# Weights-stationary products of a hybrid decoder trunk: two matmuls of 512 and 256 columns, or three of 256

## The chip, the core and the metric

One core of a Trainium2 chip runs the whole kernel. The metric is the device time of one execution in microseconds; the median of three runs is given. All inputs are in HBM at the start, and the output is in HBM at the end. The engines are TensorE (PE, whose weight loads the profile lists apart as PEld), VectorE (DVE), ScalarE (ACT), GpSimd (POOL) and SyncE (SP), which here issues the loads.

## The reference

256 tokens of width 2048 go through two layers, all in float32:

```python
for i in range(DEPTH):                       # DEPTH = 2
    hn = rms_norm(h, norm_mix[i])
    y = dsa_attention(hn, ...) if i % 2 == 0 else mlstm_mixer(hn, ...)
    h = h + y
    hn = rms_norm(h, norm_ffn[i])
    h = h + jnp.square(jax.nn.relu(hn @ ffn_w_up[i])) @ ffn_w_down[i]   # 2048 -> 8192 -> 2048
```

The attention has 16 heads of 128 with four key heads and an indexer that keeps 64 keys a token; the mLSTM has eight heads with keys and queries of 128 and values of 256. Most of the arithmetic is in the products with weights: 391 MB of them are loaded in a run.

## The kernel before

A product in float32 is made of three products of a faster type (`float32r`). Each operand is split into a high part, which that type holds exactly, and a low part, the rest. Of the four partial products high x high, high x low and low x high are kept. `weights` (L138) loads 512 rows and up to 512 columns of a weight by SyncE, in two tiles of 256 rows, and `split` (L134) makes the high part `wh` on ACT (L135) and the low part `wl` on DVE (L136). The tiles rotate: five for the loads, four each for the parts. `pair` tiles hold both parts of two blocks of 128 rows of the activations against all 256 tokens: `[P, 2 parts, 2 blocks, T]`.

There are two forms of product. `project` (L151) keeps the activations on the array and streams up to 512 columns of a weight (L166 to L168); it yields tokens on the partitions. `project_t` (L174) keeps a block of 128 x 128 of the weight on the array and streams the tokens; it yields the weight's columns on the partitions, 512 of them a call, as four blocks of 128. It is used for FFN up (two layers x four quarters x four calls) and for the mLSTM's keys and queries (four calls).

In `project_t` one call has four accumulators of a whole PSUM bank each, `[P, 2, T]`. For each of 16 blocks of rows and each of four blocks of columns, L191 streams the high and the low part of the activations side by side (512 columns) against the high part of the weight, into both halves of the bank. L193 then streams the high part of the activations (256 columns) against the low part of the weight, into the second half alone. The result is the sum of the two halves. The calls take their banks in turn from the pool `pa` (four banks, which `project` uses too) and from `px` (four banks, the helpers' pool `aux`, for transposes and small products); in the profile these accumulators are `acc` and `acx`.

The eviction adds the halves. In the FFN, `evac_up` (L457) runs for each block of 128 columns: ACT copies the second half out (L462), DVE adds the first (L463), DVE makes the squared relu (L464), and `split` makes the two parts of `hT`, ACT the high and DVE the low. In the mLSTM, `keep` (L580) does the copy and the addition (L582, L583) for `kT` and `qT`.

An FFN layer has four quarters of 2048 hidden columns: four calls of `project_t`, then four calls of `project` with 512 output columns each over the eight `hT` pairs. Each call of the latter has 16 blocks x 2 token tiles x 3 = 96 matmuls. The order of work on each engine is made by a scheduler from the program and a model of times; TensorE executes its matmuls in that order. The squares' scale (the token's factor of the norm) is put on at the very end, so that the products need not wait for the norm.

Of the kernel before, what the change touches and what calls it, by code (L numbers as in the profile page):

```python
# [9 lines left out]
F32 = mybir.dt.float32  # L10
# [27 lines left out]
def trunk_kernel(ctx: ExitStack, tc, x, norm_mix, norm_ffn, att_w_in, att_q_gain, att_k_gain,  # L38
# [16 lines left out]
    def uid(s):  # L55
        n[0] += 1
        return f"{s}_{n[0]}"

    def pair(name):
        """The exact high and low parts of two blocks of 128 rows against all tokens."""  # L60
        return lp.tile([P, 2, 2, T], F32R, tag="pair", name=uid(name))

    def t2k(shape, dt=F32, name="t2k"):
# [23 lines left out]
        nc.tensor.transpose(pg[:, :32], g, ident[:32, :32])  # L87
        nc.vector.tensor_copy(gains[:, col:col + 32], pg[:, :32])

    # TensorE's clock comes up while the first loads run.  # L90
    warm = aux()
    for _ in range(8):
        nc.tensor.matmul(warm[:, :P], zero, zero, start=True, stop=True)
# [25 lines left out]
    nc.gpsimd.memset(one0[:, 1:2], 0.0)  # L119

    def rsqrt(a, cols):
        """1/sqrt of [P, cols] (in place of a tile's values), by Newton's method from a bit-level seed."""
        seed = small([P, cols], I32, "seed")
        y = small([P, cols], F32, "y")
        u = small([P, cols], F32, "u")
        nc.vector.tensor_scalar(seed, a.bitcast(I32), 1, None, op0=ALU.logical_shift_right)
        nc.vector.tensor_scalar(y.bitcast(I32), seed, -1.0, float(0x5F3759DF), op0=ALU.mult, op1=ALU.add)
        for _ in range(3):
            nc.vector.tensor_tensor(u, a, y, op=ALU.mult)
            nc.vector.scalar_tensor_tensor(u, u, -0.5, y, op0=ALU.mult, op1=ALU.mult)  # L130
            nc.vector.scalar_tensor_tensor(y, u, 1.5, y, op0=ALU.add, op1=ALU.mult)
        return y

    def split(hi, lo, src):  # L134
        nc.scalar.copy(hi, src)  # L135
        nc.vector.tensor_tensor(lo, src, hi.bitcast(F32), op=ALU.subtract)  # L136

    def weights(src, k0, n0, width):  # L138
        """Rows k0.. (four blocks of 128) and columns n0..n0+width of a weight, as exact high and low parts."""
        parts = []  # L140
        for i in range(2):
            w = wp.tile([P, 2, 512], F32, tag="w", name=uid("w"), bufs=5)
            r0 = k0 + 256 * i
            nc.sync.dma_start(w[:, :, :width], src[r0:r0 + 256, n0:n0 + width].rearrange("(k p) f -> p k f", p=P))
            wh = wp.tile([P, 2, 512], F32R, tag="wh", name=uid("wh"), bufs=4)
            wl = wp.tile([P, 2, 512], F32R, tag="wl", name=uid("wl"), bufs=4)
            split(wh[:, :, :width], wl[:, :, :width], w[:, :, :width])
            parts.append((wh, wl))
        return parts

    def project(lhs, src, k0, n0, width, evac, before=None):  # L151
        """evac(m, psum): tokens of tile m against columns n0..n0+width. before(g) makes tiles 2g and 2g+1 of lhs."""
        acc = [pa.tile([P, 512], F32, tag="acc", name=uid("acc")) for _ in range(2)]
        nk = 2 * len(lhs)
        for g in range(nk // 4):
            if before is not None:
                before(g)
            for i, (wh, wl) in enumerate(weights(src, k0 + 512 * g, n0, width)):
                a = lhs[2 * g + i]
                for m in range(2):  # L160
                    ms = slice(m * P, (m + 1) * P)
                    o = acc[m][:, :width]
                    for j in range(2):
                        k = 4 * g + 2 * i + j
                        ah, al = a[:, 0, j, ms], a[:, 1, j, ms]
                        nc.tensor.matmul(o, ah, wh[:, j, :width], start=(k == 0), stop=False)  # L166
                        nc.tensor.matmul(o, ah, wl[:, j, :width], start=False, stop=False)  # L167
                        nc.tensor.matmul(o, al, wh[:, j, :width], start=False, stop=(k == nk - 1))  # L168
        for m in range(2):
            evac(m, acc[m][:, :width])  # L170

    turn = [0]

    def project_t(lhs, src, n0, evac):  # L174
        """evac(b, psum): block b of 128 columns from n0 on, on the partitions, against all tokens; the product
        is the sum of the two halves of psum [128, 2, T]."""
        turn[0] ^= 1
        if turn[0]:
            acc = [pa.tile([P, 2, T], F32, tag="acc", name=uid("acc")) for _ in range(4)]
        else:  # L180
            acc = [px.tile([P, 2, T], F32, tag="aux", name=uid("acx")) for _ in range(4)]
        nk = 2 * len(lhs)
        for g in range(nk // 4):
            parts = weights(src, 512 * g, n0, 512)
            for kk in range(4):
                k = 4 * g + kk
                wh, wl = parts[kk // 2]
                a = lhs[k // 2]
                for j in range(4):
                    js = slice(j * P, (j + 1) * P)  # L190
                    nc.tensor.matmul(acc[j], wh[:, kk % 2, js], a[:, :, k % 2], start=(k == 0), stop=False,  # L191
                                     skip_group_check=True)
                    nc.tensor.matmul(acc[j][:, 1], wl[:, kk % 2, js], a[:, 0, k % 2], start=False,  # L193
                                     stop=(k == nk - 1), skip_group_check=True)
        for b in range(4):
            evac(b, acc[b])

    class Norm:
        """The stationary operand of a normed stream, without its tokens' factors; those come out of finish()."""

        def __init__(self, col):
            self.col = col
# [7 lines left out]
                                     accum_out=self.ss[:, m, c:c + 1])  # L210

        def chunk(self, c, squares=None):
            """squares: None for this chunk's own, True for those of all chunks, False for none."""
            for i in (2 * c, 2 * c + 1):
                p = aux()
                for j in range(2):
# [27 lines left out]
            return self  # L244

    def rope_cols(slab, v, heads, half, c0):
        """Turn the first 2*half columns of each head of v [P, 2, heads, d]."""
        rot = 2 * half
        shape = [P, 2, heads, rot]
        a = slab(shape, "ropa")  # L250
# [8 lines left out]
        nc.vector.tensor_tensor(v[:, :, :, :rot], a, b, op=ALU.add)  # L259

    def add_to_h(norm, r2=None):
        """Adds a product's columns to the stream, and hands them to the next norm."""

        def at(c):
            def evac(m, p):
# [8 lines left out]
        return at  # L274

    def slabs(pool, bufs):
        """Tiles of one phase: bufs by tag."""
        return lambda shape, name, tag=None: pool.tile(shape, F32, tag=tag or name, bufs=bufs[tag or name],
                                                       name=uid(name))

    # ---------------------------------------------------------------- attention
    def attention(nm, nxt, pool):
        slab = slabs(pool, {"v": 1, "kT": 1, "qT": 3, "hn": 3, "sq": 2, "ropa": 1, "ropb": 1, "lg": 5, "pT": 3, "sc": 4})
        lhs = nm.lhs
# [86 lines left out]
            bias.append(b)  # L371

        def heads_t(dst, gain):
            """evac of four heads of 128 columns: normed, turned and transposed into dst [P, 4, T]."""
            o = slab([P, 2, 4, DH], "hn")

            def evac(m, p):
# [71 lines left out]
            project(oT, w_ao, 0, 512 * c, 512, at(c))  # L449
        nxt.finish()  # L450

    # ---------------------------------------------------------------- feed-forward
    def ffn(nm, up, down, nxt, last=False):
        for q in range(4):
            hT = []

            def evac_up(b, p):  # L457
                if b % 2 == 0:
                    hT.append(pair("hT"))
                a = hT[-1]  # L460
                u = t2k([P, 2, T], F32, "u")
                nc.scalar.copy(u[:, 0], p[:, 1])  # L462
                nc.vector.tensor_tensor(u[:, 0], p[:, 0], u[:, 0], op=ALU.add)  # L463
                nc.vector.scalar_tensor_tensor(u[:, 1], u[:, 0], 0.0, u[:, 0], op0=ALU.max, op1=ALU.mult)  # L464
                split(a[:, 0, b % 2], a[:, 1, b % 2], u[:, 1])

            for c in range(4):
                project_t(nm.lhs, up, q * 2048 + 512 * c, evac_up)
# [13 lines left out]
        if nxt is not None:  # L482
            nxt.finish()

    # ---------------------------------------------------------------- mLSTM
    def mlstm(nm, nxt, pool):
        slab = slabs(pool, {"go": 4, "mkT": 1, "mqT": 1, "mv": 2, "num": 2, "gT": 1, "row": 1, "et": 2, "pt": 2,
                            "mjunk": 2, "hs": 3})
# [4 lines left out]
        HD = MH * MV  # L493

        def put_o(m, c0, p, width):
            """sigmoid(o) times the heads' gain, for columns c0.. of o."""
            done = 0
            while done < width:
                c = c0 + done
# [17 lines left out]
        e = small([P, 2, MH], F32, "e")  # L517
        nc.vector.scalar_tensor_tensor(e, fg, -1.0, fg, op0=ALU.mult, op1=ALU.min)
        nc.scalar.activation(e, e, AF.Exp)
        # log(1 + e) as log(u) + (e - (u - 1)) / u, with u the rounded 1 + e.  # L520
        u = small([P, 2, MH], F32, "u1")
        ru = small([P, 2, MH], F32, "ru")
        nc.vector.tensor_scalar(u, e, 1.0, None, op0=ALU.add)
# [18 lines left out]
        nc.vector.tensor_tensor_scan(mm, cs, one0[:, 1:2].to_broadcast([MH, T]), 0.0, op0=ALU.max, op1=ALU.max)  # L542
        negm = slab([MH, T], "negm", "hs")
        nc.vector.scalar_tensor_tensor(negm, cum, -1.0, mm, op0=ALU.mult, op1=ALU.subtract)
        # Rows 0.. and 32.. of parts are the exact high and low parts of -mm; pick adds the two of one head.
        parts = pool.tile([40, T], F32R, tag="parts", bufs=1, name="parts")
        pick = cp.tile([40, MH], F32R, name="pick")
        nc.vector.tensor_tensor(pick, ident[:40, :MH], ident[:40, 32:32 + MH], op=ALU.add)
# [27 lines left out]
        for half in range(2):  # L576
# [2 lines left out]

            def keep(dst):  # L580
                def evac(b, p):
                    nc.scalar.copy(dst[:, b], p[:, 1])  # L582
                    nc.vector.tensor_tensor(dst[:, b], p[:, 0], dst[:, b], op=ALU.add)  # L583
                return evac

            project_t(lhs, w_ml, MK0 + 512 * half, keep(kT))
# [84 lines left out]


def _rope_table():
    """By position: [cos cos | -sin sin] of the attention's rotation, then the indexer's."""
    import numpy as np
    cols = []
    for rot in (RC, IC):
# [29 lines left out]
```

## Time and profile before

| | |
|---|---|
| Median of 3 runs | 2126.35 us (2126.17 to 2127.8) |
| Profiled execution, first to last instruction (span) | 2124.9 us |
| PE busy | 2115.0 us, 100%, 10748 records |
| PEld busy | 1810.0 us, 85%, 10748 records |
| DVE, ACT busy | 1242.6 us (58%), 1010.1 us (48%) |
| DMA | 393.09 MB, mean 185 GB/s |

The profile is of one execution, whose own time is known as its span; the runs' times include what lies around that. Times in the rows are microseconds from the span's start, and the means of one instruction are in ns. Matmuls are pipelined: the record of one is longer than the step from its start to the next one's, and its end is modelled. Steps between starts, and counts, are therefore what a rate is read from. A float32 matmul that is not of the split type shows as two records.

### The profile page before, as it was taken

The page shows a single profiled execution, that of the slowest core. Times are in us where ns is not written, and L with a number is a line of the kernel's source. Part 1 is how long each engine was busy: PE and PEld are TensorE (multiplying, and loading weights), DVE is VectorE, ACT ScalarE, POOL GpSimd, SP SyncE. Part 2 cuts the span into 40 slices and gives each one's busy share as a digit, 9 for nine tenths or more (in the row PEclk, how much of TensorE's full clock was granted, in tenths as well). Part 3 has the DMA queues.
Part 4 walks back from the last instruction along what each step waited for, and adds up shares of the span by engine and source line. Part 5 has one row for each costly group of instructions (what it writes and reads, how often), then busy time and mean ns, then how long its engine had stood idle before and what let it go on. Part 6 is the DMA issues. An engine that isn't in the chain of part 4 may idle for free.

```text
span 2124.9 us, 27918 instructions
## 1 busy us (share of the span) xinstructions
PE 2115.0 (100%) x10748; PEld 1810.0 (85%) x10748; DVE 1242.6 (58%) x1866; ACT 1010.1 (48%) x1400; POOL 14.0 (1%) x20
## 2 busy tenths in 40 slices
PE   9999999999999999999999999999999999999999
PEld 8988888888888888888999888888888888888887
DVE  5697656645555565565654565656555555654654
ACT  6556554534443443444554554545434434443542
POOL 0000000000000000000011000000000000000000
PEclk9999999999999999999999999999999999999999
DMA  7665356656656656665566555466566666666664
GB/s 234 188 180 151 119 178 188 188 193 191 191 191 187 198 189 196 190 189 188 166 185 209 171 165 176 161 188 188 193 194 189 191 194 189 191 193 191 189 205 140
DMA packets 207926, 393.09 MB, mean 185 GB/s; under 512 B 12784, under 2 KB 29616, under 8 KB 207792
## 3 DMA queue, kind: packets, MB, share of 16 engines
q1 hardware_dynamic: 207744, 391.29, 60.4%
q8 instruction: 84, 1.38, 0.2%
q14 instruction: 50, 0.41, 0.1%
q10 hardware_dynamic: 48, 0.02, 0.0%
HBM read 389.16 MB, written 2.10 MB: 184 GB/s over the span
## 4 chain that ended last, share of the span: by engine, by line
PE 99%; ACT 0%; DMA 0%; DVE 0%; issue 0%; SPq 0%; DVEq 0%
PE acc L167 19%; PE acc L168 19%; PE acc L166 19%; PE acc L191 13%; PE acx L191 13%; PE acc L193 6%; PE acx L193 6%; PE aux L219 1%; PE aux L412 0%; PE aux L440 0%; PE aux L620 0%; PE aux L349 0%; DMA w<-in_att_w_in_dram 0%; PE aux L611 0%; PE aux L396 0%; PE aux L645 0%
## 5 line engine op out<-in xcount | busy, mean ns | idle before, releaser
L136 DVE TENSOR_TENSOR wl<-w,wh 128x1024 fp32r<-128x1024 f32 (+3 forms) x752 | 907.1, 1207 | 820.6 <-ACT wh L135 819.5
L135 ACT CAST wh<-w 128x1024 fp32r<-128x1024 f32 (+3 forms) x752 | 777.6, 1035 | 970.6 <-PE acc L168 576.6
L191 PE MATMUL acc<-xT,wh 128*128 128x512 f32 x1152 | 401.1, 394 | 0.0
L191 PE MATMUL acx<-xT,wh 128*128 128x512 f32 x1152 | 399.9, 393 | 0.0
L166 PE MATMUL acc<-wh,hT 128*128 128x512 f32 x1024 | 398.7, 389 | 0.0
L167 PE MATMUL acc<-wl,hT 128*128 128x512 f32 x1024 | 398.7, 389 | 0.0
L168 PE MATMUL acc<-wh,hT 128*128 128x512 f32 x1024 | 398.4, 389 | 0.0
L193 PE MATMUL acc<-xT,wl 128*128 128x256 f32 x1152 | 318.9, 278 | 0.0
L193 PE MATMUL acx<-xT,wl 128*128 128x256 f32 x1152 | 318.4, 278 | 0.0
L191 PEld LDWEIGHTS acx<-xT,wh 128*128 128x128 f32 x1152 | 215.7, 187 | 49.3
L191 PEld LDWEIGHTS acc<-xT,wh 128*128 128x128 f32 x1152 | 215.4, 188 | 48.9
L166 PEld LDWEIGHTS acc<-wh,hT 128*128 128x128 f32 x1024 | 192.2, 188 | 40.0
L168 PEld LDWEIGHTS acc<-wh,hT 128*128 128x128 f32 x1024 | 192.2, 188 | 39.7
L167 PEld LDWEIGHTS acc<-wl,hT 128*128 128x128 f32 x1024 | 192.2, 188 | 39.5
L193 PEld LDWEIGHTS acc<-xT,wl 128*128 128x128 f32 x1152 | 216.5, 188 | 1.3
L193 PEld LDWEIGHTS acx<-xT,wl 128*128 128x128 f32 x1152 | 216.2, 188 | 0.3
L166 PE MATMUL acc<-wh,xT 128*128 128x512 f32 (+3 forms) x576 | 212.4, 372 | 2.3 <-ACT xT L226 2.3
L167 PE MATMUL acc<-wl,xT 128*128 128x512 f32 (+3 forms) x576 | 212.7, 371 | 0.0
L168 PE MATMUL acc<-wh,xT 128*128 128x512 f32 (+3 forms) x576 | 211.9, 371 | 0.0
L166 PEld LDWEIGHTS acc<-wh,xT 128*128 128x128 f32 x576 | 108.1, 188 | 15.1 <-ACT xT L226 2.5
L167 PEld LDWEIGHTS acc<-wl,xT 128*128 128x128 f32 x576 | 108.3, 188 | 12.9 <-issue 0.7
L168 PEld LDWEIGHTS acc<-wh,xT 128*128 128x128 f32 x576 | 108.3, 188 | 12.8 <-issue 0.3
(204 smaller groups left out, 1308.1 us busy)
## 6 DMA issues: line engine op xcount, KB each, us to landing
w<-in_ffn_w_up_dram SPq DMA_DIRECT2D x256, 512.0 KB, 3.8
w<-in_ffn_w_down_dram SPq DMA_DIRECT2D x256, 512.0 KB, 4.3
w<-in_ml_w_in_dram SPq DMA_DIRECT2D x64, 512.0 KB, 3.8
w<-in_att_w_in_dram SPq DMA_DIRECT2D x48, 512.0 KB, 4.4
w<-in_att_w_out_dram SPq DMA_DIRECT2D x32, 512.0 KB, 4.4
w<-in_ml_w_out_dram SPq DMA_DIRECT2D x32, 512.0 KB, 3.7
w<-in_ml_w_in_dram SPq DMA_DIRECT2D x32, 412.0 KB, 3.7
w<-in_att_w_in_dram SPq DMA_DIRECT2D x24, 368.0 KB, 3.6
```

What stands on the lines that cost most here:

```text
L135: nc.scalar.copy(hi, src)
L136: nc.vector.tensor_tensor(lo, src, hi.bitcast(F32), op=ALU.subtract)
L166: nc.tensor.matmul(o, ah, wh[:, j, :width], start=(k == 0), stop=False)
L167: nc.tensor.matmul(o, ah, wl[:, j, :width], start=False, stop=False)
L168: nc.tensor.matmul(o, al, wh[:, j, :width], start=False, stop=(k == nk - 1))
L191: nc.tensor.matmul(acc[j], wh[:, kk % 2, js], a[:, :, k % 2], start=(k == 0), stop=False, skip_group_check=True)
L193: nc.tensor.matmul(acc[j][:, 1], wl[:, kk % 2, js], a[:, 0, k % 2], start=False, stop=(k == nk - 1), skip_group_check=True)
L219: nc.tensor.transpose(p[:, j * T + m * P:j * T + (m + 1) * P], h[:, m, k * P:(k + 1) * P], ident)
```

## The change

`project_t` gives each block of 128 columns a half bank, 256 columns, so that a call has two accumulators in place of four, always from `pa`. All three partial products go into the same 256 columns: the wide matmul is parted into high x high and high x low, both with the same block of the weight on the array, and the third follows. Only the first matmul into a bank has the start flag. `evac` is called twice a call with a whole bank, which holds two finished blocks. The FFN eviction copies the bank by ACT, squares it by DVE, and splits it into one `pair`; the mLSTM's copies it. The additions are gone. Comments and docstrings are removed too, which changes nothing that runs.

```diff
-    turn = [0]
-
     def project_t(lhs, src, n0, evac):
-        turn[0] ^= 1
-        if turn[0]:
-            acc = [pa.tile([P, 2, T], F32, tag="acc", name=uid("acc")) for _ in range(4)]
-        else:
-            acc = [px.tile([P, 2, T], F32, tag="aux", name=uid("acx")) for _ in range(4)]
+        acc = [pa.tile([P, 2, T], F32, tag="acc", name=uid("acc")) for _ in range(2)]
         nk = 2 * len(lhs)
         for g in range(nk // 4):
             parts = weights(src, 512 * g, n0, 512)
...
                 a = lhs[k // 2]
+                ah, al = a[:, 0, k % 2], a[:, 1, k % 2]
                 for j in range(4):
                     js = slice(j * P, (j + 1) * P)
-                    nc.tensor.matmul(acc[j], wh[:, kk % 2, js], a[:, :, k % 2], start=(k == 0), stop=False,
-                                     skip_group_check=True)
-                    nc.tensor.matmul(acc[j][:, 1], wl[:, kk % 2, js], a[:, 0, k % 2], start=False,
-                                     stop=(k == nk - 1), skip_group_check=True)
-        for b in range(4):
-            evac(b, acc[b])
+                    o = acc[j // 2][:, j % 2]
+                    hi, lo = wh[:, kk % 2, js], wl[:, kk % 2, js]
+                    nc.tensor.matmul(o, hi, ah, start=(k == 0 and j % 2 == 0), stop=False, skip_group_check=True)
+                    nc.tensor.matmul(o, hi, al, start=False, stop=False, skip_group_check=True)
+                    nc.tensor.matmul(o, lo, ah, start=False, stop=(k == nk - 1), skip_group_check=True)
+        for b in range(2):
+            evac(2 * b, acc[b])
...
             def evac_up(b, p):
-                if b % 2 == 0:
-                    hT.append(pair("hT"))
-                a = hT[-1]
                 u = t2k([P, 2, T], F32, "u")
-                nc.scalar.copy(u[:, 0], p[:, 1])
-                nc.vector.tensor_tensor(u[:, 0], p[:, 0], u[:, 0], op=ALU.add)
-                nc.vector.scalar_tensor_tensor(u[:, 1], u[:, 0], 0.0, u[:, 0], op0=ALU.max, op1=ALU.mult)
-                split(a[:, 0, b % 2], a[:, 1, b % 2], u[:, 1])
+                nc.scalar.copy(u, p)
+                nc.vector.scalar_tensor_tensor(u, u, 0.0, u, op0=ALU.max, op1=ALU.mult)
+                a = pair("hT")
+                split(a[:, 0], a[:, 1], u)
+                hT.append(a)
...
             def keep(dst):
                 def evac(b, p):
-                    nc.scalar.copy(dst[:, b], p[:, 1])
-                    nc.vector.tensor_tensor(dst[:, b], p[:, 0], dst[:, b], op=ALU.add)
+                    nc.scalar.copy(dst[:, b:b + 2], p)
                 return evac
```

## Rows read from the trace of the kernel before

**Rows 1.** The page's head: span, busy time by engine, granted clock in 40 slices

```profile
span 2124.9 us, 27918 instructions
PE 2115.0 (100%) x10748; PEld 1810.0 (85%) x10748; DVE 1242.6 (58%) x1866; ACT 1010.1 (48%) x1400; POOL 14.0 (1%) x20
...
PEclk9999999999999999999999999999999999999999
```

**Rows 2.** The chain that ended last, shares of the span by engine and line

```profile
PE 99%; ACT 0%; DMA 0%; DVE 0%; issue 0%; SPq 0%; DVEq 0%
PE acc L167 19%; PE acc L168 19%; PE acc L166 19%; PE acc L191 13%; PE acx L191 13%; PE acc L193 6%; PE acx L193 6%; PE aux L219 1%; PE aux L412 0%; PE aux L440 0%; PE aux L620 0%; PE aux L349 0%; DMA w<-in_att_w_in_dram 0%; PE aux L611 0%; PE aux L396 0%; PE aux L645 0%
```

**Rows 3.** Waits, PE's longest (two of four) and ACT's: total us, times, longest

```profile
PE acc L166 <- ACT xT L226: 2.3, 1, 2.3
PE aux L440 <- ACT pT L438: 2.2, 2, 2.0
...
ACT wh L135 <- PE acc L168: 576.6, 371, 3.8
ACT wh L135 <- PE acc L191: 180.9, 112, 4.1
ACT wh L135 <- PE acx L191: 167.6, 106, 4.0
```

**Rows 4.** Timeline of PE, FFN up and down of layer 0: start, us, instruction

```profile
701.73 0.40 PE L191 MATMUL acx<-xT,wh 128*128 128x512 f32 x1
701.97 0.28 PE L193 MATMUL acx<-xT,wl 128*128 128x256 f32 x1
702.08 0.39 PE L191 MATMUL acx<-xT,wh 128*128 128x512 f32 x1
...
723.92 0.40 PE L191 MATMUL acc<-xT,wh 128*128 128x512 f32 x1
...
746.11 0.40 PE L191 MATMUL acx<-xT,wh 128*128 128x512 f32 x1
...
768.29 0.40 PE L166 MATMUL acc<-wh,hT 128*128 128x512 f32 x1
768.53 0.39 PE L167 MATMUL acc<-wl,hT 128*128 128x512 f32 x1
768.76 0.39 PE L168 MATMUL acc<-wh,hT 128*128 128x512 f32 x1
...
855.34 0.39 PE L191 MATMUL acc<-xT,wh 128*128 128x512 f32 x1
```

**Rows 5.** Groups of instructions: busy us, mean ns | idle before

```profile
L191 PE MATMUL acc<-xT,wh 128*128 128x512 f32 x1152 | 401.1, 394 | 0.0
L191 PE MATMUL acx<-xT,wh 128*128 128x512 f32 x1152 | 399.9, 393 | 0.0
...
L193 PEld LDWEIGHTS acc<-xT,wl 128*128 128x128 f32 x1152 | 216.5, 188 | 1.3
...
L167 PEld LDWEIGHTS acc<-wl,hT 128*128 128x128 f32 x1024 | 192.2, 188 | 39.5
L166 PEld LDWEIGHTS acc<-wh,hT 128*128 128x128 f32 x1024 | 192.2, 188 | 40.0
```

**Rows 6.** Timeline of PE, 368-column products: first and last of 102

```profile
38.14 0.33 PE L168 MATMUL acc<-wh,xT 128*128 128x368 f32 x1
...
54.97 0.33 PE L167 MATMUL acc<-wl,xT 128*128 128x368 f32 x1
```

**Rows 7.** Timeline of PE and PEld, the two places with four L193 in line

```profile
1259.74 1.09 PE L191 MATMUL acx<-xT,wh 128*128 128x512 f32 x4
1260.67 0.63 PE L193 MATMUL acx<-xT,wl 128*128 128x256 f32 x4
1261.14 0.40 PE L191 MATMUL acx<-xT,wh 128*128 128x512 f32 x1
...
1263.46 0.64 PE L193 MATMUL acx<-xT,wl 128*128 128x256 f32 x4
1263.93 0.40 PE L191 MATMUL acx<-xT,wh 128*128 128x512 f32 x1
...
1260.44 0.66 PEld L193 LDWEIGHTS acx<-xT,wl 128*128 128x128 f32 x4
1261.03 0.19 PEld L191 LDWEIGHTS acx<-xT,wh 128*128 128x128 f32 x1
```

**Rows 8.** Busy time in the ten us with most PE records

```profile
89.90:99.90 10.00, 10.00 (x79) 7.94 (x78) 5.27 (x10) 6.11 (x10) 0.00 (x0) 1.00 0.56 166
```

**Rows 9.** Timeline of PE, the indexer's short matmuls

```profile
94.79 2.06 PE L349 MATMUL aux<-kiT,qiT 64*128 64x128 f32 x32
96.78 0.50 PE L166 MATMUL acc<-wh,xT 128*128 128x512 f32 x1
```

**Rows 10.** Groups by shape: the FFN eviction, and nearest forms of 512 elements

```profile
L464 DVE SCALAR_TENSOR_TENSOR u<-u 128x256 f32<-128x256 f32 x128 | 50.8, 418 | 0.0
L136 DVE TENSOR_TENSOR hT<-u,hT 128x256 fp32r<-128x256 f32 x128 | 48.3, 420 | 0.0
L135 ACT CAST hT<-u 128x256 fp32r<-128x256 f32 x128 | 46.0, 414 | 17.1 <-DVE u L464 17.1
L270 DVE SCALAR_TENSOR_TENSOR h<-acc,r,h 128x512 f32<-128x512 f32 x56 | 39.4, 744 | 0.1
L463 DVE TENSOR_TENSOR u<-acc,u 128x256 f32<-128x256 f32 x64 | 25.7, 421 | 0.0
L462 ACT COPY u<-acc 128x256 f32<-128x256 f32 x64 | 23.0, 372 | 12.8 <-PE acc L193 12.8
L136 DVE TENSOR_TENSOR hsT<-aux,hsT 128x512 fp32r<-128x512 f32 x8 | 5.5, 684 | 2.3 <-ACT hsT L135 2.3
L135 ACT CAST hsT<-aux 128x512 fp32r<-128x512 f32 x8 | 4.7, 586 | 6.1 <-PE aux L645 6.0
L397 ACT COPY qT<-aux 128x512 f32<-128x512 f32 x8 | 4.6, 589 | 2.2 <-PE aux L396 2.2
```

**Rows 11.** Instructions on the tile mkT, an mLSTM eviction: min/median/max ns

```profile
L583 DVE TENSOR_TENSOR mkT<-acc,mkT x8: 414/419/424, 1147.6 to 1250.4; 128x256 f32<-128x256 f32 x8
```

## The prediction

> **What bounds the kernel now.** I read the page's head first: TensorE (PE) is busy 100% of a span of 2124.9 us with a granted clock of nine tenths or more in every slice, so at its upper level of 2.4 GHz [rows 1]. The chain that ended last is 99% PE, over a third of it in the lines that change, L191 and L193 [rows 2]. PE's waits are four in the whole run, the two longest 2.3 and 2.2 us, 5.9 us in all, and none is for an eviction (L462, L463, L582, L583) or for an accumulator bank [rows 3]. The bound is therefore the rate at which PE streams matmuls, and the other engines have slack: ACT waits for PE to give back weight buffers for hundreds of us [rows 3]. A busy share says nothing of that rate, since a PE record (392 ns) is longer than the step to the next one. I took the rates from the timeline, as distances between starts.
>
> **The rate of a weights-stationary call.** One call is 4 groups x 4 blocks x 4 columns of blocks = 64 steps, each a 512-column matmul (L191) and a 256-column one (L193). Three calls in a row start at 701.73, 723.92 and 746.11, and the product after them at 768.29 [rows 4]: 66.56 us for 192 steps, 346.7 ns a step. Within a step some 0.24 us pass from the wide start to the narrow one and 0.11 from there to the next wide one [rows 4]. Steps in the whole kernel are 1152 + 1152 = 2304 [rows 5]: 2304 x 346.7 = 798.8 us.
>
> **What a matmul costs beside its columns.** Two widths of the token-stationary product give it. Four calls of 96 matmuls of 512 columns run from 768.29 to 855.34 [rows 4]: 87.05 us / 384 = 226.7 ns; the columns at 2.4 GHz take 213.3, and 13.4 are over. 101 matmuls of 368 columns lie between 38.14 and 54.97 [rows 6]: 166.6 ns, columns 153.3, and 13.3 over. So the cost is columns / 2.4 + 13.3 ns at either width. The step of the weights-stationary call obeys it too: 768 columns are 320.0 ns, and two matmuls add 26.7, which makes the 346.7 that was read. This is the main finding: each of these matmuls, whatever its width, carries a fixed 13.3 ns.
>
> The Trainium skill (TensorE: Matmul & The Clock Gate, "Back-to-back issue gap") gives a warm gap of N / 2.4 + 2.5 ns. The trace disagrees, with 13.3 in place of 2.5 [rows 4, 6], and I go by the trace. By the page's figure the estimate for the change would be 2304 x 2.5 = +5.8 us.
>
> **The change, part by part.**
>
> *Matmuls.* The wide matmul against [ah al] becomes two of 256 columns, and the third stays at 256 but goes to the same columns. Columns stay 768. Matmuls go from two to three a step, loads too: consecutive matmuls on one stationary block still each load it, as L166 and L167 do today with the same `ah` (1024 loads for either line) [rows 5], and the step from L166 to L167 is no shorter than that from L167 to L168 [rows 4]. By the rule above a step becomes 3 x (106.7 + 13.3) = 360.0 ns. That is 13.3 x 2304 = +30.7 us.
>
> The disputed price is a 256-column matmul behind another one. There are two short runs of four: 1260.67 to 1261.14 and 1263.46 to 1263.93 [rows 7], 0.47 us / 4 = 117.5 ns. A step of 3 x 117.5 = 352.5 would add 5.8 x 2304 = 13.4 us. But such runs also shift time onto their neighbours: the four wide and four narrow ones from 1259.74 to 1261.14 took 1.40 us, against 4 x 0.3467 = 1.387 in the usual order. So I take the long averages (120.0) and keep 117.5 as the low end. From above, the densest 10 us of the trace hold 79 PE records [rows 8], 126.6 ns each; a step of 380 would add 33.1 x 2304 = 76 us. Nothing shows a longer step as needed, so this is the high end. 120.0 lies nearer the low one.
>
> *Banks.* The accumulators take two banks of `pa` in place of four of `pa` or `px` in turn; two are left for the call behind, and `px` is free for the helpers. PE waits for no bank now [rows 3], so there is little to win; the 5.9 us of all PE waits bound it, and I count nothing. A call's banks are needed again two calls later, some 23 us, and an eviction takes under 3.
>
> *Eviction.* Per block of 128 columns, now: ACT copy 372, DVE add 421, DVE square 418, ACT cast 414, DVE subtraction 420 ns [rows 10]. After, per two blocks: one copy (nearest row 589), one square (at most the 744 of L270), one cast (586), one subtraction (684) [rows 10]. DVE goes from 2 x 1259 = 2518 to at most 1428 per two blocks, some 70 us less over 64; ACT from 1572 to 1175. The four mLSTM calls lose their additions likewise (eight of 0.42 us for `kT` [rows 11] and as many for `qT`). All this is hidden now under 22.2 us of matmuls per call, and no PE wait names it, so it is worth nothing. If that cover were gone, one eviction in line would be about 2.6 us per call. ACT's and DVE's next work, splitting weights, waits for PE anyway (ACT 925 us for L168 and L191) [rows 3], and the DMAs behind it wait for those buffers; none of it comes to PE sooner.
>
> *Queue order.* A bank is now ready after both of its blocks. Nothing on SP or POOL moves, no DMA is added. The last eviction of an FFN quarter feeds the seventh and eighth pair of `hT`, needed only in the fourth group of the next product, after 72 matmuls of 226.7 ns = 16.3 us, against two evictions of about 2.6 us in line. Nothing becomes late.
>
> *Sum.* The profiled execution has 2124.9 us of span [rows 1], and the median of the runs, 2126.35, lies 1.45 over that, for what stands around the span. The span becomes 2124.9 + 30.7 = 2155.6, the time 2126.35 + 30.7 = **2157 us**, slower by 1.4%.
>
> **The rivals.**
>
> 1. *The narrow run is cheaper than the rule.* For it: the four-long runs at 117.5 ns [rows 7]. Against it: both fitted widths and the present step. It gives 2126.35 + 13.4 = 2140.
>
> 2. *The repeated block costs no second load*, and the 13.3 ns belong to the load. Then a step is 320 + 2 x 13.3, as before, and the time stays: 2126. For it: the first two matmuls use one block. Against it: the two load counts of L166 and L167, and their equal steps [rows 4, 5].
>
> 3. *Faster: the halves cost what the narrow matmul behind a wide one shows.* From 701.97 to 702.08 it takes 0.11 us [rows 4]. If 0.11 were the whole price of 256 contiguous columns, and the wide matmul paid the rest for its two-part moving operand, a step would be 330 ns: -16.7 x 2304 = -38.5 us, 2088. It decides once a narrow matmul costs under 115.6 ns, a third of 346.7. Against it: two 256s in a row never show that [rows 7], and the contiguous 512 carries the same 13.3 [rows 4].
>
> 4. *Weight loads become the bound.* PEld is busy 1810 us, 85% [rows 1], and a load record is 188 ns [rows 5], longer than a narrow matmul. 2304 more such loads end to end would add 433 us, to 2243, over the span. If loads had to stand end to end, a step would last 564 ns and the kernel some 500 us longer. Against it: the four loads of a run took 0.66 us from the first start to the last end, not 4 x 0.188 = 0.75, and the next began before that end [rows 7]; records overlap. A milder form, in which a long stream falls to the densest 10 us of the trace [rows 8], gives 2126.35 + 76 = 2202. Two us at twice the present rate exist (L349, 32 in 2.0 us [rows 9]), but none of 22 us.
>
> The Trainium skill (Perfetto Trace Analysis, "Identifying the Most-Contended Engine") counts the LDWEIGHTS busy share as the measure of how little headroom TensorE has, not matmul busy time. By it this change eats the last headroom; the overlap in [rows 7] is why I give it no more.
>
> **How the numbers follow.** A change of 0.2%, 4.3 us, is about what can be told from none here. Chances: forecast 0.68, rival 1 0.13, rival 2 0.08, rival 3 0.05, rival 4 0.06. Slower is the forecast, 1 and 4: 0.87. The likeliest case's own range is 2150 to 2163 (13.3 by 10% or so, and a few us for waits). Taking in rival 1 to its low side, and the lower part of rival 4, gives **2137 to 2168**, which leaves out rivals 2 and 3 and most of 4, about 0.18.
>
> **What would show it.** In the trace after: three matmul lines of 256 columns with 2304 each, 6912 in all; as many loads; a call of 64 steps lasting 23.04 us in place of 22.19; products with 512 columns at 226.7 ns as before; DVE busy lower by about 70 us; PE's wait total still some 6 us. Wrong would be a call of 22.2 us or less, fewer loads than matmuls, or a PE wait on an eviction of a few us a call.

## The result, and the profile after

The changed kernel takes 2154.73 us (median of four runs, 2153.5 to 2156.7) against 2126.41 before: a ratio of 1.0132, with a 95% interval of 1.0118 to 1.0146. It is slower by 28.3 us, where 30.7 was forecast.

The page's head, for the changed kernel:

```profile
span 2151.7 us, 32116 instructions
## 1 busy us (share of the span) xinstructions
PE 2142.8 (100%) x13052; PEld 1938.3 (90%) x13052; DVE 1194.0 (55%) x1594; ACT 994.7 (46%) x1264; POOL 14.0 (1%) x20
...
PE 99%; ACT 0%; DMA 0%; DVE 0%; issue 0%; SPq 0%; DVEq 0%
PE acc L167 19%; PE acc L166 19%; PE acc L168 19%; PE acc L189 13%; PE acc L190 13%; PE acc L188 13%; PE aux L215 1%; PE aux L408 0%; PE aux L436 0%; PE aux L613 0%; PE aux L345 0%; DMA w<-in_att_w_in_dram 0%; PE aux L604 0%; PE aux L392 0%; ACT lg L418 0%; PE aux L438 0%
```

Beside [rows 1, 2]: PE has 2304 matmuls and 2304 loads more, is as full as before, and is still 99% of the chain, so what a step gained went into the span. DVE and ACT are busy for 48.6 and 15.4 us less, and nothing came of it. The groups of the new lines (line, engine, operation, shapes, count, busy us, mean ns, idle before) and PE's waits:

```profile
L188 PE MATMUL acc<-xT,wh 128*128 128x256 f32 x2304 | 652.6, 283 | 0.0
L189 PE MATMUL acc<-xT,wh 128*128 128x256 f32 x2304 | 652.4, 283 | 0.0
L190 PE MATMUL acc<-xT,wl 128*128 128x256 f32 x2304 | 652.2, 283 | 0.0
L189 PEld LDWEIGHTS acc<-xT,wh 128*128 128x128 f32 x2304 | 442.3, 192 | 0.5
L188 PEld LDWEIGHTS acc<-xT,wh 128*128 128x128 f32 x2304 | 442.2, 192 | 0.3
L190 PEld LDWEIGHTS acc<-xT,wl 128*128 128x128 f32 x2304 | 442.3, 192 | 0.0
...
L455 ACT COPY u<-acc 128x512 f32<-128x512 f32 x64 | 37.3, 583 | 39.5 <-PE acc L190 39.5
L456 DVE SCALAR_TENSOR_TENSOR u<-u 128x512 f32<-128x512 f32 x64 | 44.1, 689 | 19.0 <-ACT u L455 19.0
```

```profile
PE aux L436 <- ACT pT L434: 2.2, 2, 2.0
PE acc L166 <- ACT xT L222: 1.5, 1, 1.5
PE aux L93 <- DVE zero L76: 1.0, 1, 1.0
PE acc L167 <- DVE wl L136: 0.4, 1, 0.4
```

L189 uses the block that L188 has just used and loads it again, 2304 times. The wait total is 5.1 us, and no wait is for an eviction or a bank. The rate is read from starts, as before: PE's timeline over one FFN quarter (start, us, instruction).

```profile
504.99 0.28 PE L188 MATMUL acc<-xT,wh 128*128 128x256 f32 x1
505.10 0.28 PE L189 MATMUL acc<-xT,wh 128*128 128x256 f32 x1
505.22 0.28 PE L190 MATMUL acc<-xT,wl 128*128 128x256 f32 x1
505.34 0.28 PE L188 MATMUL acc<-xT,wh 128*128 128x256 f32 x1
...
597.14 0.40 PE L166 MATMUL acc<-wh,hT 128*128 128x512 f32 x1
```

Four calls (a quarter), 256 steps, take 597.14 - 504.99 = 92.15 us: 360.0 ns a step. A 256-column matmul in a long stream costs 120.0 ns, the value of the long averages, and not the 117.5 of the runs of four [rows 7]. The token-stationary product behind it, 384 matmuls of 512 columns, keeps its 226.7 ns (597.14 to 684.21, where the next quarter starts).

The product 2304 x 13.3 = 30.7 us is over the 28.3 between the medians and the 26.8 between the two spans. Half a microsecond of the difference is the step before: a whole quarter of the kernel before goes from 679.49 to 768.29, 88.80 us or 346.9 ns a step and not 346.7, so a step gained 13.1 ns, 30.2 us in all. Two us of the gap to 26.8 are the start: the first 368-column matmul begins at 32.58 us in the profiled execution before and at 30.62 in the one after. Busy time and granted clock by ten us, the kernel before and then the changed one (PE, PEld, DVE, ACT, POOL, clock, DMA share, GB/s).

```profile
0.00:10.00 10.00, 6.69 (x30) 5.79 (x31) 2.23 (x5) 5.28 (x9) 1.96 (x12) 0.98 0.82 254
10.00:20.00 10.00, 10.00 (x46) 8.37 (x46) 8.19 (x13) 9.41 (x23) 0.00 (x0) 0.85 1.04 372
```

```profile
0.00:10.00 10.00, 7.42 (x32) 6.25 (x33) 2.65 (x6) 5.69 (x10) 1.97 (x12) 1.00 0.78 256
10.00:20.00 10.00, 10.00 (x53) 8.40 (x52) 8.78 (x17) 10.00 (x25) 0.00 (x0) 1.00 1.06 371
```

In the execution profiled before, PE had stood idle for 3.3 of the first 10 us and the clock was partly at its lower level in the next 10 (mean 0.85). In the one after, it stood idle for 2.6 and the clock stayed up, and PE was 9 matmuls further after 20 us (85 against 76). A run of the changed matmuls below (e1) again has a mean of 0.83 there. This belongs to the execution and not to the change; it is the size of error that a single span carries here. The rest of the way to the 28.3 between the medians lies in executions that have no trace.

### The profile page after: what moved, and what is told of

It reads as the page before. It is cut to its first block, busy times and chain, and to the rows that moved or that the text cites. A ratio compares the mean times of both kernels' runs of the same rounds, so it can differ in the third digit from the quotient of the medians.

```text
span 2151.7 us, 32116 instructions
## 1 busy us (share of the span) xinstructions
PE 2142.8 (100%) x13052; PEld 1938.3 (90%) x13052; DVE 1194.0 (55%) x1594; ACT 994.7 (46%) x1264; POOL 14.0 (1%) x20
## 4 chain that ended last, share of the span: by engine, by line
PE 99%; ACT 0%; DMA 0%; DVE 0%; issue 0%; SPq 0%; DVEq 0%
PE acc L167 19%; PE acc L166 19%; PE acc L168 19%; PE acc L189 13%; PE acc L190 13%; PE acc L188 13%; PE aux L215 1%; PE aux L408 0%; PE aux L436 0%; PE aux L613 0%; PE aux L345 0%; DMA w<-in_att_w_in_dram 0%; PE aux L604 0%; PE aux L392 0%; ACT lg L418 0%; PE aux L438 0%
## 5 line engine op out<-in xcount | busy, mean ns | idle before, releaser
L188 PE MATMUL acc<-xT,wh 128*128 128x256 f32 x2304 | 652.6, 283 | 0.0
L189 PE MATMUL acc<-xT,wh 128*128 128x256 f32 x2304 | 652.4, 283 | 0.0
L190 PE MATMUL acc<-xT,wl 128*128 128x256 f32 x2304 | 652.2, 283 | 0.0
L189 PEld LDWEIGHTS acc<-xT,wh 128*128 128x128 f32 x2304 | 442.3, 192 | 0.5
L188 PEld LDWEIGHTS acc<-xT,wh 128*128 128x128 f32 x2304 | 442.2, 192 | 0.3
L190 PEld LDWEIGHTS acc<-xT,wl 128*128 128x128 f32 x2304 | 442.3, 192 | 0.0
L455 ACT COPY u<-acc 128x512 f32<-128x512 f32 x64 | 37.3, 583 | 39.5 <-PE acc L190 39.5
L456 DVE SCALAR_TENSOR_TENSOR u<-u 128x512 f32<-128x512 f32 x64 | 44.1, 689 | 19.0 <-ACT u L455 19.0
```

The lines of the kernel that those rows point to most:

```text
L188: nc.tensor.matmul(o, hi, ah, start=(k == 0 and j % 2 == 0), stop=False, skip_group_check=True)
L189: nc.tensor.matmul(o, hi, al, start=False, stop=False, skip_group_check=True)
L190: nc.tensor.matmul(o, lo, ah, start=False, stop=(k == nk - 1), skip_group_check=True)
L455: nc.scalar.copy(u, p)
L456: nc.vector.scalar_tensor_tensor(u, u, 0.0, u, op0=ALU.max, op1=ALU.mult)
```

## The experiments

**The matmuls alone.** Is it the third matmul, or what it is packed with (one accumulator, half the banks, the new eviction)?

```diff
# e1, from the kernel before
-    nc.tensor.matmul(acc[j], wh[:, kk % 2, js], a[:, :, k % 2], start=(k == 0), ...)
+    for s in range(2):
+        nc.tensor.matmul(acc[j][:, s], wh[:, kk % 2, js], a[:, s, k % 2], start=(k == 0 and s == 0), ...)
```

> The wide matmul is parted in two of 256 columns, each into its own half of the bank; four banks a call, the additions and the eviction stay as before. Theory (a fixed 13.3 ns for each matmul): a step of 360 ns, 2304 x 13.3 = 30.7 us over the kernel before, ratio 1.0132 to 1.0145, as the whole change. Rival (the loss comes from three passes into the same 256 columns, from half the banks or from the eviction): 346.7 ns and 2126 us, ratio 1.000.

Measured: 2155.78 us, ratio 1.0129 (1.0114 to 1.0144). PE's timeline, first step of a quarter and what follows the last:

```profile
507.97 0.40 PE L192 MATMUL acc<-xT,wh 128*128 128x256 f32 x2
508.20 0.28 PE L194 MATMUL acc<-xT,wl 128*128 128x256 f32 x1
...
600.12 0.40 PE L166 MATMUL acc<-wh,hT 128*128 128x512 f32 x1
```

Again 92.15 us for 256 steps. The parted matmul alone has the whole loss; accumulating into the same columns and sharing banks cost nothing.

**The eviction alone.**

```diff
# e2, from the kernel before; the evictions themselves as in the changed kernel
-        for b in range(4):
+        for b in range(0, 4, 2):
             evac(b, acc[b])
```

> The matmuls and the four banks of the kernel before with the new eviction: two whole banks a call are copied, squared and split, no addition. The other two banks and the sum of the halves are left out. Theory (eviction is hidden under the matmuls): a step of 346.7 ns, the time of the kernel before within 0.1%, though DVE is busy some 70 us less. Rival (the lighter eviction or earlier weights give PE something back): 2 to 10 us less.

Measured: 2127.54 us against 2127.81, ratio 0.9998 (0.9989 to 1.0008). The same quarter runs from 503.35 to 592.15 on PE's timeline, 88.80 us or 346.9 ns a step. A lighter eviction returns nothing.

**The eviction three times over**, for its cover from the other side:

```diff
# e6, from the changed kernel
+    for _ in range(3):
         nc.scalar.copy(u, p)
         nc.vector.scalar_tensor_tensor(u, u, 0.0, u, op0=ALU.max, op1=ALU.mult)
```

> The changed kernel with copy and square of the FFN eviction done three times for each bank: 2 x (0.583 + 0.689) = 2.54 us more in line for each bank, 163 us more over 64 banks on ACT and DVE. Theory (hidden: a call of 23 us has slack on both): the time of the changed kernel within 0.2%. Rival (the eviction is near the path, by weights or banks that come later): 5 to 160 us more.

Measured: 2154.3 us, ratio 1.0124 (1.0108 to 1.0139), that of the changed kernel. The groups of the repeated copy and square, x192 in place of x64:

```profile
L456 ACT COPY u<-acc 128x512 f32<-128x512 f32 x192 | 105.6, 585 | 39.5 <-PE acc L190 39.5
...
L457 DVE SCALAR_TENSOR_TENSOR u<-u 128x512 f32<-128x512 f32 x192 | 126.5, 687 | 19.0 <-ACT u L456 19.0
```

Some 70 us more on ACT and 80 on DVE are swallowed whole.

**The order within a step**, so that no two neighbours share a block:

```diff
# e4, from the changed kernel
-    matmul(o, hi, al, ...); matmul(o, lo, ah, ...)
+    matmul(o, lo, ah, ...); matmul(o, hi, al, ...)
```

> The changed kernel with the second and third matmul of a step exchanged, so that no two consecutive ones use the same block of the weight. Theory (each matmul pays its own load and its own 13.3 ns, whatever came before): 360.0 ns, the time of the changed kernel, ratio to before 1.0132 or so. Rival (the second use of a block is cheaper in part): slower than the changed kernel by up to 2304 x 13.3 = 31 us, ratio up to 1.028.

Measured: 2156.4 us, ratio 1.0128 (1.0111 to 1.0145); a quarter of FFN up runs from 508.77 to 600.92, 92.15 us. Using a block twice in a row saves nothing, and losing that costs nothing.

**Narrower parts.** The fixed part had been fitted at 368 and 512 columns and held at 256. How far down?

```diff
# e3, from the kernel before, c = 192 (384 and 128 columns) or 160 (320 and 192)
+    for s in (slice(0, c), slice(c, T)):
+        nc.tensor.matmul(acc[j][:, :, s], wh[:, kk % 2, js], a[:, :, k % 2, s], ...)
```

> The kernel before with the wide matmul parted in 384 and 128 columns, so three matmuls of 384, 128 and 256 a step. Theory in its plain form (columns / 2.4 + 13.3 ns at any width): 173.3 + 66.7 + 120.0 = 360 ns, 2155 us. Rival (a matmul can't follow faster than its successor's load, which a 256-column one just covers, so 107 to 120 ns is a floor): 173.3 + 107 to 120 + 120 = 400 to 413 ns, 2304 x (53 to 67) = 123 to 153 us over before, 2250 to 2280 us.

> The kernel before with the wide matmul parted in 320 and 192 columns: 320, 192 and 256 a step. Plain theory: 146.7 + 93.3 + 120.0 = 360 ns, 2155 us. Rival (a floor of 107 to 120 ns by the load): 146.7 + 107 to 120 + 120 = 374 to 387 ns, 63 to 92 us over before, 2189 to 2219 us.

Measured: 2262.54 us (ratio 1.0637, 1.0606 to 1.0668) and 2194.38 us (1.0316, 1.0287 to 1.0346). PE's timeline of the first (x2 are the wide part and the narrow one):

```profile
518.05 0.39 PE L192 MATMUL acc<-xT,wh 128*128 128x384 f32 x2
518.28 0.33 PE L194 MATMUL acc<-xT,wl 128*128 128x256 f32 x1
518.45 0.40 PE L192 MATMUL acc<-xT,wh 128*128 128x384 f32 x2
...
622.17 0.40 PE L166 MATMUL acc<-wh,hT 128*128 128x512 f32 x1
```

104.12 us / 256 = 406.7 ns a step, and 376.6 in the second (510.18 to 606.60). The plain rule falls here and the floor holds. With 173.3 and 120.0 put down for the other two, 113.4 ns are left for the 128-column matmul; with 146.7 and 120.0, 110.0 for the 192-column one. All three forms have three matmuls and 768 columns. The loads in the same trace show the floor itself:

```profile
518.23 0.19 PEld L194 LDWEIGHTS acc<-xT,wl 128*128 128x128 f32 x1
518.33 0.31 PEld L192 LDWEIGHTS acc<-xT,wh 128*128 128x128 f32 x2
```

In a quarter of the changed kernel each load starts 2 to 5 ns after the matmul ahead of its own. Here the load for the 256-column matmul does so too, with the narrow one, but the next load comes only 108.3 ns after it (mean of 251 in the quarter, none under 107; 108.3 in the second form as well), when the 256-column matmul has already started. In the starts of PE the lost time therefore stands behind that matmul (0.17 us from 518.28 to 518.45), and the wide and the narrow one together take 0.23; the 113.4 and 110.0 are what a difference leaves, and 108 is the floor that was read. The 120.0 ns of a 256-column matmul lie just above it.

**Half a load.** Is that floor the load of the next block, and what do the 13.3 ns go with?

```diff
# e7, from the changed kernel and from e3 with 384 and 128
-    js = slice(j * P, (j + 1) * P)
+    w = P if k == 0 else P // 2          # output rows :w too
+    js = slice(j * P, j * P + w)
```

> The changed kernel, three matmuls of 256 columns a step, but from the second block of rows on only 64 of the 128 columns of a block are put on the array: a load half as wide, the same moving columns. The products of the other 64 columns are left out. If the fixed 13.3 ns go with the matmul: 360 ns, 2155 us. If they go with the load (128 columns of it, or its handing over): 320 to 345 ns in 15 of 16 steps, 32 to 86 us less, 2068 to 2122 us.

> The kernel with 384, 128 and 256 columns a step (406.7 ns, 2262.5 us), with the same half load from the second block of rows on, the products of the other 64 columns left out. If the floor of some 113 ns found for the narrow matmul is the time of its successor's load: it falls to half, the narrow one costs 66.7 and the step 360 ns or less, 2155 us or less. If it is a floor of the matmul itself: 406.7 ns and 2262 us.

Measured: 2112.4 us (0.993, 0.9908 to 0.9953) and 2133.66 us (1.003, 1.0018 to 1.0043), both where they were put if the load sets the price. PE's timeline of the first, and its loads:

```profile
501.89 0.28 PE L189 MATMUL acc<-xT,wh 128*128 128x256 f32 x1
...
589.16 0.28 PE L191 MATMUL acc<-xT,wl 128*64 128x256 f32 x1
589.27 0.40 PE L166 MATMUL acc<-wh,hT 128*128 128x512 f32 x1
```

```profile
L189 PEld LDWEIGHTS acc<-xT,wh 128*64 128x64 f32 x2160 | 290.4, 134 | 0.0
```

87.38 us / 256 = 341.3 ns a step. One step in 16 still has full blocks at 360.0, so the others take (16 x 341.3 - 360.0) / 15 = 340.1: 20.1 over the columns in place of 40.0. Half a load leaves half of what was over, with the moving columns unchanged (the output is half as wide as well, which this run can't part from the load). The narrow version goes from 406.7 to 350.6 (505.60 to 595.36), 346.9 in the steps with half loads. Its loads:

```profile
511.96 0.13 PEld L195 LDWEIGHTS acc<-xT,wl 128*64 128x64 f32 x1
512.02 0.28 PE L195 MATMUL acc<-xT,wl 128*64 128x256 f32 x1
512.02 0.25 PEld L193 LDWEIGHTS acc<-xT,wh 128*64 128x64 f32 x2
```

They start some 60 ns apart behind the narrow matmul, and again each with the matmul ahead of its own: the floor goes with the width of the load. But 26.9 ns are over the columns here and 20.1 in the even form, with as many half loads and columns. So 6.7 ns, a third of 20.1, is no fixed price of a half load.

**A load of another type.** The same words read as bfloat16, upper halves only:

```diff
# e5, from the changed kernel (three) and from the kernel before (two); e8 is "two" with the wide one parted in 384 and 128
+    def b16(t): return t.bitcast(mybir.dt.bfloat16)      # operands as b16(x)[..., 1::2]
```

> The changed kernel with both operands of the weights-stationary products read as bfloat16: the upper halves of the same words, every second element. Columns, loads and counts are unchanged; the lower 16 bits of both operands are left out. If the 13.3 ns belong to every matmul whatever its type: 360 ns, 2155 us. If they belong to the split float32 type: between 320 and 330 ns, 2304 x 30 to 40 = 69 to 92 us less than the changed kernel, 2063 to 2086 us. If they come from the load alone and a 16-bit load is shorter: the same as the second.

> The kernel before with the operands of the weights-stationary products read as bfloat16 in the same way, two matmuls a step; the lower 16 bits are left out. If the 13.3 ns belong to every matmul: 346.7 ns, 2126 us, and 31 us under the run with three. If they belong to the type: between 320 and 325 ns, 50 to 61 us under the kernel before, and within 12 us of the run with three: then parting the wide matmul costs next to nothing in that type.

> The kernel before with bfloat16 reads and the wide matmul parted in 384 and 128 columns; the lower 16 bits are left out. Load records in bfloat16 are 97 ns in place of 188. If the floor is the load's and a 16-bit load is shorter: about the step of the bfloat16 runs, 338 to 347 ns, 2108 to 2128 us. If the floor is the same: 53 to 60 in place of 113 is not reached, 380 to 390 ns, 2205 to 2230 us.

Measured: 2110.21 us with three (0.9921, 0.9892 to 0.995), 2108.28 with two (0.9912, 0.9883 to 0.994), 2110.46 with 384 and 128 (0.9921, 0.9892 to 0.9949). I read the rate inside a quarter, from the second step to the last (254 steps), since a start next to another type is displaced. PE's timeline of the run with three, and its loads:

```profile
501.93 0.27 PE L191 MATMUL acc<-xT,wh 128*128 128x256 bf16 x1
...
588.29 0.27 PE L191 MATMUL acc<-xT,wh 128*128 128x256 bf16 x1
```

```profile
L191 PEld LDWEIGHTS <-wh 128*128 128x128 bf16 x2304 | 222.9, 97 | 40.5 <-issue 2.4 <-ACT go L499 0.2
```

86.36 us / 254 = 340.0 ns with three; 338.3 with two (502.63 to 588.56); 340.0 with 384 and 128 (504.00 to 590.36), where no floor is left, as was stated for a shorter load. None of the prices stated before the runs with two and three was met: what is over the columns neither stays nor goes. With three it is 20.0, as with the half loads, beside load records half as long; with two it is 18.3. So parting the wide matmul costs 1.7 ns in this type, not 13.3, and most of what is over is no price of a matmul or of its load. A 256-column matmul takes 113.3 there, which leaves 225.0 for the 512-column one beside it: 6.7 and 11.7 over the columns, more for more columns.

That leaves a rival for float32r which no run decides. A 256-column matmul takes 113.4 ns under half a load, 113.3 in bfloat16 and 120.0 under a full load. If 113.3 were its own time, half of the 226.7 for 512 columns, and a full load held it up to 120.0, the change would lose the same 13.3 ns a step (3 x 120.0 against 226.7 + 120.0) with no fixed part at all. Against it stand the 166.6 ns at 368 columns [rows 6], where the same share of 226.7 would be 162.9. A step of two matmuls, 512 and 256 columns, under half loads would part the two: 333 ns with 6.7 a load, 340 by the rival. Shown is that an added matmul with its full load costs 13.3 ns here; what the 13.3 are made of stays open.

**A version that would beat both?** The finding pointed at cheaper loads: leave the large product as it was, and read only the two small ones as bfloat16.

```diff
# e9, from the kernel before: the low x high products in both forms
-    nc.tensor.matmul(o, ah, wl[:, j, :width], ...); nc.tensor.matmul(o, al, wh[:, j, :width], ...)
+    nc.tensor.matmul(o, b16(ah), b16(wl[:, j, :width]), ...); nc.tensor.matmul(o, b16(al), b16(wh[:, j, :width]), ...)
-    nc.tensor.matmul(acc[j][:, 1], wl[:, kk % 2, js], a[:, 0, k % 2], ...)
+    nc.tensor.matmul(acc[j][:, 1], b16(wl[:, kk % 2, js]), b16(a[:, 0, k % 2]), ...)
```

> The kernel before with only the operands of the two small partial products (low x high, high x low) read as bfloat16, in both forms of product; their lower 16 bits are left out, and the high x high product stays as it was. If the fixed part goes with the load and a 16-bit load leaves 6.6 ns in place of 13.3 also here: 2304 narrow matmuls save 6.7 ns, 15 us, and the 3712 of the token-stationary products 1.8 to 6.7 ns each (the wide one in the bfloat16 run with two cost about 225 in place of 226.7 to 230), 7 to 25 us: 2086 to 2105 us. Rival (the part goes with the type of the neighbours, or a change of type between matmuls costs something): 2126 us or more.

Measured: 2189.14 us, ratio 1.0287 (1.0273 to 1.0301): the rival. PE and PEld on the timeline, in a weights-stationary call:

```profile
699.73 0.48 PE L194 MATMUL acc<-xT,wh 128*128 128x512 f32 x1
700.05 0.10 PEld L196 LDWEIGHTS <-wl 128*128 128x128 bf16 x1 [0.16 <-issue]
700.05 0.29 PE L196 MATMUL acc<-xT,wl 128*128 128x256 bf16 x1
700.05 0.20 PEld L194 LDWEIGHTS acc<-xT,wh 128*128 128x128 f32 x1
700.09 0.47 PE L194 MATMUL acc<-xT,wh 128*128 128x512 f32 x1
700.40 0.10 PEld L196 LDWEIGHTS <-wl 128*128 128x128 bf16 x1
```

The bfloat16 load begins only when its own matmul is about to, 0.32 us after the wide one started; in the kernel before, the load of the narrow matmul begins with the wide one:

```profile
701.73 0.40 PE L191 MATMUL acx<-xT,wh 128*128 128x512 f32 x1
701.74 0.19 PEld L193 LDWEIGHTS acx<-xT,wl 128*128 128x128 f32 x1
```

The step becomes 0.36 us, and three token-stationary matmuls of 512 take 0.700 us (610.04 to 612.84 for four such groups) in place of 0.680 [rows 4]. Here the changes of type cost more than the shorter loads save. No version here beats the kernel before with its products whole.

## Why the prediction was right

*The rate of a stream, not busy shares.* The step was forecast at 360.0 ns and is 360.0; the quarter at 4 x 23.04 = 92.16 us and is 92.15. The price came from two widths of another product and the present step [rows 4, 6], and held for a sequence that the trace before hardly has. The two runs of four [rows 7] would have given 13.4 us; they were rightly kept as an end of the range.

*"Whatever its width" was too much.* The rule was read at 512 and 368 columns and carried down to 256. It holds there and fails at 192 and 128 (e3). No row showed the floor of 108 ns, so it was in part luck that the change stopped at 256: parted at 192 columns, the same rule would have missed by 36 us (67 us over the kernel before, not 31). And in bfloat16 an added matmul costs 1.7 ns (e5): the fixed part belongs, at most, to this type and this load.

*No saving for a repeated block (rival 2).* It had two halves. That the repeated block costs no second load is false: every matmul loads again, whatever came before (e4, and the counts of L188 and L189). That the 13.3 ns belong to the load is true as far as a shorter load takes 20 of the 40 ns over the columns away (e7, e5); the other 20 are not explained. The prediction called the 13.3 a cost of each matmul; with one load per matmul the change can't tell the two apart.

*Banks and eviction at nothing.* Shown from both sides: e1 has neither and loses all of it, e2 has the eviction and gains nothing, e6 adds 150 us of eviction work and loses nothing. Only the size of the relief was off: DVE's busy time fell by 48.6 us, not 70. The sum took record lengths one after another, but short DVE records overlap: the 128 squares of 418 ns [rows 10] are 53.5 us long together and kept DVE busy for 50.8. All DVE records together are 79 us shorter; 80.5 us of them overlapped before and 50.2 after.

*Rivals 1 and 3* fall with the 120.0 ns of a long stream. *Rival 4* was near: load records do not stand end to end (three of 192 ns overlap in a step of 360), but in e3 a full load came no sooner than 107 to 108 ns after the one before it, and 128 or 192 columns meet that. The Trainium skill (TensorE: Matmul & The Clock Gate, "LDWEIGHTS (loading the stationary operand)") gives columns / 1.2 ns for a load, by which an estimate for 128 columns is 107 ns. The 108.3 of e3 agree. For 64 columns the estimate is 53; no run here shows a half load held up, and the closest starts, some 60 ns apart, do not contradict it. The same page ("Weight-path perf modes — Fast Weight Load (FWL) and DoubleRow") says that a faster weight load is on for 128 weights of a type other than FP32; the load records of 97 ns in bfloat16 and 192 in float32r fit that if float32r counts as FP32.

*The 2.5 ns of the Trainium skill (TensorE: Matmul & The Clock Gate, "Back-to-back issue gap").* The measured 28.3 us are not the 5.8 of that figure; the trace decided rightly. The section itself gives the figure for an isolated matmul, and says that in a stream where each matmul brings its load both set the spacing.

## What to carry to other kernels

Where PE is the bound, price a matmul by the distance between starts at two widths, in the type that it has: the slope is the columns, and what is over was paid again here for each added matmul with its load, so parting a wide matmul cost it again though the columns stayed the same. Don't carry the price to widths below those that it was read at. Count stationary loads, not only columns, and keep the moving side wider than the next load takes: at 192 and 128 columns of this type the load's 108 ns were the price, while at 256 the sum read at 368 and 512 still gave the time. Relief on engines that PE does not wait for was worth nothing (e2, e6).

## What the runs showed of the hardware that was not expected

A step of three 256-column matmuls of float32r stood 40.0 ns over its columns with loads of 128 columns and 20.1 with loads of 64; in bfloat16 it stood 20.0 over, and two matmuls of 512 and 256 columns 18.3 (340.0 and 338.3 ns). Loads of 128 float32r columns came no sooner than 107 to 108 ns after one another in the narrow forms, whose steps of the same 768 columns took 406.7 and 376.6 ns; loads of 64 columns came after some 60. Alternating float32r and bfloat16 made a step of 768 columns in two matmuls 360 ns long, as long as three matmuls of float32r alone.
